# A second plain pair at the start of each feed-forward layer, and token sums formed in place

## The chip, the cores and the metric

The kernel runs on one core of a Trainium2 chip. The metric is device time in microseconds (us) of one execution. Engines are named as in the profile: PE multiplies matrices, DVE, ACT and POOL work on tiles, SP issues DMAs.

## The reference

A block of two layers over 1024 tokens of width 1024, in float32. Layer 0 mixes tokens (spatial gating and a convolution), layer 1 is dilated attention; behind each stands the feed-forward layer that the change touches:

```python
def conv_ffn(x, norm_g, w_up, conv_w, conv_b, w_down):
    h = rms_norm(x, norm_g)
    u = causal_dwconv(h @ w_up, conv_w, conv_b)      # width 3 along tokens
    gate, val = jnp.split(u, 2, axis=-1)             # 2 x 2816 channels
    return x + (jax.nn.silu(gate) * val) @ w_down
```

## The kernel before

**One product in three.** Every float32 matrix is held as a high and a low part (`hi_of`: ACT's cast; `lo_of`: a subtraction, mostly on DVE), and a product of 128 x 128 weights with 512 tokens is three matmuls into one PSUM bank: high by high, high weights by low tokens, low weights by high tokens. The third is the first that needs the low part of the weights. All DVE and POOL instructions are issued through one helper, so that they have line L115; hi_of has L183.

**The up stage.** The 2816 gate and 2816 value channels are worked through in 22 pairs of 128 gate and 128 value channels. The normed activations `hT` have four blocks, token half t by half b of the width 1024 (`hT.block(t, b)`), each of a high and a low tile (`hTh`, `hTl`). A pair is a product of 2 x 2 blocks of weights (gate, value by b) with 2 x 2 blocks of tokens. It exists in two forms:

- *plain* (`plain`, `up_units`): all eight block products, as four units (gate or value, by token half) of 24 matmuls each into a `psu` bank. It needs the two weight tiles `wr` split into `wh` and `wl`, and `hT`.
- *seven products* (`Pair`, Strassen's scheme in Winograd's form): `p12` (two products with `hT.block(0, ...)`, banks `psb` and `psa`), `p6`, `p57`, `p4` with token sums T[2], T[1] and T[3], T[4], and `p3` with `hT.block(1, 1)`. Each product is 12 matmuls (lines L929, L930, L932). It needs weight sums, made by `plan` in steps (gate parts a1; four POOL sums s12, s3, s4; then the parts of s12, s3, s4), three snapshots `sn` of a bank on ACT and three additions on DVE.

The token sums are formed once a layer out of the transposed norms `xr` (`hT.raw`): `t_sums(i)` adds up token tile i with tile i + 4, and `t_parts(i, m)` splits sum m of that tile into T[m] (`t1h`, `t1l` and so on; the low part of T[4] on POOL, the others on DVE).

Then `Conv.put` forms the bias and the last tap on ACT (`y`, L810) and the other taps on DVE out of the bank; a bank of the first token half is held until the second half's taps are done. `gate` multiplies Silu(gate) by value and stores it.

**What sets the order.** The program is written as one sequence for all engines: a `Ticker` counts steps (a step follows every 6 matmuls), `after(n, f)` puts `f` n steps later, and `until` runs steps until something has been issued. Each engine carries out its own instructions in the order written, and waits on semaphores. So moving an `after` moves an instruction in its engine's queue and nothing else.

At the start of a layer the last norms (8 token tiles, `norm_tile`) are still under way. Before, pair 0 is plain and pairs 1 and 2 are the first of the seven-product form: pair 0's units of the first token half, `p12` of pair 1, all four tiles' `t_sums`, pair 0's units of the second half, `p12` of pair 2, then the sums' products of pairs 1 and 2 in turn; from pair 3 on a loop in which `p4` and `p3` of a pair follow `p12` of the next.

Of the kernel before, what the change touches and what calls it, by code (L numbers as in the profile page):

```python
# [21 lines left out]
HALF = 512  # L22
# [7 lines left out]
NPAIR = D_FF // P  # L30
# [30 lines left out]
LEADS = (4, 6)  # L61

START_AT = 8


class Ticker:
# [56 lines left out]
def block_kernel(ctx, tc, io, out):  # L123
# [5 lines left out]
    tk = Ticker()  # L129
    vec = Meter(nc.vector, 0.12, 1.06e-3)  # L130
    pool = Meter(nc.gpsimd, 0.12, 2.25e-3)
    tk.hooks.append(lambda: (vec.step(1.28), pool.step(1.3)))
    after, tick = tk.after, tk.tick
# [16 lines left out]
    def stile(shape=(P, D), dt=F32, name="s"):  # L150
        return spool.tile(list(shape), dt, tag="s", name=nm(name))
# [30 lines left out]
    def hi_of(hi, src):  # L182
        nc.scalar.copy(hi, src)  # L183

    def lo_of(lo, src, hi, eng=None):
        (eng or vec).tensor_tensor(lo, src, f32v(hi), op=ALU.subtract)
# [206 lines left out]
    def up_units(hT, ws, outs, done=None, early=False):  # L393

        if early:
            yield from first_half(hT, ws, outs)
            for n in range(len(ws)):
                after(1, lambda n=n: done(n, 0))
        for t in range(1 if early else 0, 2):
            x = hT.wait(t)  # L400
            for n, (wh, wl) in enumerate(ws):
                whv = wh.rearrange("p (k c) -> p k c", k=KT)
                wlv = wl.rearrange("p (k c) -> p k c", k=KT)
                ps = bank("psu")
                outs[(n, t)] = ps
                for k in range(KT):
                    mm3(ps, (whv[:, k, :], wlv[:, k, :]), x(k), k == 0, k == KT - 1)
                    if k == KT - 1 and done is not None:
                        after(1, lambda n=n, t=t: done(n, t))
                    if k % 2 == 1:  # L410
                        yield

    def drive(gen):
        for _ in gen:
            tick()
# [380 lines left out]
    def ffn_up(l, acts):  # L796
        fcw = param("fcw", [P, 2 * NPAIR, 3], l)
        fcb = param("fcb", [P, 2 * NPAIR], l)
        raws = {}
        first = []  # L800

        def fetch(j):
            if j < NPAIR:
                raws[j] = (stile(name="wr"), stile(name="wr"))
                for n in range(2):
                    src = io["w_up"][l, j + n * NPAIR].rearrange("p k c -> p (k c)")
                    nc.sync.dma_start(raws[j][n], src)
# [45 lines left out]
            return part.rearrange("p (k c) -> p k c", k=4)  # L853


        def start():
            fetch(0)

            def part():
                hi, lo = stile(dt=F32R, name="wh"), stile(dt=F32R, name="wl")  # L860
                raw = raws[0][len(first)]
                hi_of(hi, raw)
                after(1, lambda hi=hi, lo=lo, raw=raw: lo_of(lo, raw, hi))
                first.append((hi, lo))
            after(START_AT, part)
            after(START_AT + 2, part)
            after(START_AT + 4, lambda: fetch(1))

        def plain(hT):
            tk.until(lambda: len(first) == 2 and 1 in raws)  # L870
            cv, outs = Conv(0), {}
            return up_units(hT, first, outs, lambda n, t: cv.put(n, t, outs[(n, t)]))


        prep = {}
# [4 lines left out]
            after(1, lambda: lo_of(lo, src, hi))  # L880
            return hi, lo

        def plan(j, lead, lag=0):


            if j >= NPAIR:
                return
            o = prep[j] = {}

            def two(t):  # L890
                return t.rearrange("p (b c) -> p b c", b=2)

            def gate_parts():
                g = two(raws[j][0])
                o["a1"] = split_s(g)

            def sums():
                g, v = two(raws[j][0]), two(raws[j][1])
                s12, s4 = stile([P, 2, HALF], name="s12"), stile([P, 2, HALF], name="s4")
                o["s12r"], o["s4r"] = s12, s4  # L900
                pool.tensor_tensor(s12[:, 0, :], v[:, 0, :], v[:, 1, :], op=ALU.add)
                pool.tensor_tensor(s12[:, 1, :], s12[:, 0, :], g[:, 0, :], op=ALU.subtract)
                pool.tensor_tensor(v[:, 0, :], g[:, 0, :], v[:, 0, :], op=ALU.subtract)
                pool.tensor_tensor(s4[:, 0, :], g[:, 1, :], s12[:, 1, :], op=ALU.subtract)

            def s12_parts():
                o["s12"] = split_s(o["s12r"])

            def s3_parts():
                o["s3"] = split_s(two(raws[j][1]))  # L910

            def s4_parts():
                hl = stile([P, 2, HALF], F32R, name="w4")
                hi_of(hl[:, 0, :], o["s4r"][:, 0, :])
                after(1, lambda: lo_of(hl[:, 1, :], o["s4r"][:, 0, :], hl[:, 0, :]))
                o["s4"] = hl
            after(lead - 6 + lag // 3, gate_parts)
            after(lead - 5 + lag, sums)
            after(lead + 1 + lag, s12_parts)
            after(lead + 5 + lag, s3_parts)  # L920
            after(lead + 9 + lag, s4_parts)

        def product(ps, a, b, first, last):
            (ah, al), (bh, bl) = a, b
# [11 lines left out]
        T, sums = {}, {}  # L936
        tails = deque()

        def t_sums(hT, i):

            r0, r1 = hT.raw[i], hT.raw[i + 4]
            ta = stile([P, 2, HALF], name="ta")
            vec.tensor_tensor(ta[:, 0, :], r1[:, 0, :], r0[:, 0, :], op=ALU.subtract)
            vec.tensor_tensor(ta[:, 1, :], r1[:, 1, :], ta[:, 0, :], op=ALU.subtract)
            pool.tensor_tensor(r1[:, 0, :], r1[:, 1, :], r1[:, 0, :], op=ALU.subtract)
            pool.tensor_tensor(r0[:, 1, :], r0[:, 1, :], ta[:, 1, :], op=ALU.subtract)
            sums[i] = {1: ta[:, 0, :], 2: ta[:, 1, :], 3: r1[:, 0, :], 4: r0[:, 1, :]}

        def t_parts(i, m):

            if m not in T:
                T[m] = operand(f"t{m}")
            hi, lo = T[m]
            c = slice(i * P, (i + 1) * P)
            v = sums[i][m].rearrange("p (k t) -> p k t", k=4)
            split(v, hi[:, :, c], lo[:, :, c], pool if m == 4 else None)

        class Pair:
# [7 lines left out]
                self.sn[key] = stile([P, HALF], name="sn")  # L966
                nc.scalar.copy(self.sn[key], self.b)  # L967

            def p12(self, late=0):
                self.b, self.a = bank("psb"), bank("psa")  # L970
                product(self.b, self.part("a1", 0), self.hT.block(0, 0), True, True)
                after(1, lambda: self.snap("p1"))
                product(self.a, self.part("a1", 1), self.hT.block(0, 1), True, True)

                def c11():
                    vec.tensor_tensor(self.a, self.a, self.sn["p1"], op=ALU.add)
                    after(1, lambda: self.cv.put(0, 0, self.a))
                after(1 + late, c11)

            def p6(self):  # L980
                product(self.b, self.part("s12", 1), T[2], False, True)
# [28 lines left out]
                after(1, c12)  # L1010

        def run(hT):

            gen = plain(hT)
            plan(1, 8, 10)
            after(4, lambda: fetch(2))
            for _ in range(8):
                next(gen)
                tick()
            one, two = Pair(1, hT), None  # L1020
            plan(2, 12, 5)
            after(18, lambda: fetch(3))
            one.p12()
            hT.wait(1)
            for i in range(4):
                after(1 + i, lambda i=i: t_sums(hT, i))
            for n, m in enumerate((2, 1, 3, 4)):
                for i in range(4):
                    after(4 + (4 * n + i) * 3 // 4, lambda i=i, m=m: t_parts(i, m))
            drive(gen)  # L1030
            two = Pair(2, hT)
            two.p12(5)
            plan(3, 16)
            one.p6()
            one.p57()
            two.p6()
            one.p4()
            one.p3()
            two.p57()
            tails.extend((two.p4, two.p3))  # L1040
            for j in range(3, NPAIR):
                plan(j + 1, 14)
                after(4, lambda j=j: fetch(j + 2))
                if j == 3:
                    fetch(4)
                p = Pair(j, hT)
                p.p12()
                while tails:
                    tails.popleft()()
                p.p6()  # L1050
                p.p57()
                tails.extend((p.p4, p.p3))
            return tails
# [527 lines left out]
    hT = Normed()  # L1581
# [133 lines left out]
```

## Time and profile before

| | us |
|---|---|
| three runs | 2329.06 (median), 2328.94, 2331.13 |
| the profiled execution | 2330.07 |
| its span in the trace | 2328.3 |

Rows of instructions read: start, duration, engine, line, operation, output<-inputs (buffer numbers left out), shapes, count; in brackets how long the engine had been idle before and what ended that. A matmul's duration is its latency; matmuls overlap, so PE's pace is the distance between starts. In the tables of windows the columns are the length, then the busy time and number of instructions of each engine, the granted clock of PE (1.00 is full speed), and the DMA engines' share and rate.

### The profile page before, as it was taken

What the parts mean: (1) busy time and instruction counts of PE and PEld (TensorE: products, weight loads), DVE (VectorE), ACT (ScalarE), POOL (GpSimd) and SP (SyncE); (2) the same over time, 40 slices, a digit from 0 to 9 for tenths busy, and PEclk for the clock granted to TensorE, in tenths of its full rate; (3) what the DMA queues carried; (4) which work ended last, traced back from release to release, by engine and by line L of the source; (5) the groups of instructions that cost most, each with busy time, mean ns of one, the idle gap of its engine ahead of it and who ended that gap; (6) DMA issues with size and microseconds to landing.
All of it is one profiled execution on the core that took longest, in us unless ns stands there. A gap on an engine that the chain in (4) does not pass through costs nothing. (4 is left out here: it accounts for less than half of the span.)

```text
span 2328.3 us, 28663 instructions
## 1 busy us (share of the span) xinstructions
PE 2235.6 (96%) x10616; PEld 1863.7 (80%) x10616; DVE 1585.4 (68%) x2530; ACT 1078.1 (46%) x1648; POOL 461.9 (20%) x387
## 2 busy tenths in 40 slices
PE   7998888999999999999999999999899999999998
PEld 6886676888888888887888888787678888888887
DVE  6977759877777743425777777776887777774352
ACT  4356265444444533323555555654544444454140
POOL 1022136233333002010000000122633333310000
PEclk9999889999999999999999999999999999999999
DMA  5389611222222563525344444723122222247260
GB/s 200 87 145 220 167 76 52 83 89 87 87 85 68 178 247 130 205 89 132 97 112 111 114 118 118 226 64 110 46 90 82 82 82 82 82 156 278 71 245 36
DMA packets 87884, 281.23 MB, mean 121 GB/s; under 512 B 12352, under 2 KB 12736, under 8 KB 87744
## 3 DMA queue, kind: packets, MB, share of 16 engines
q1 hardware_dynamic: 80976, 254.91, 33.4%
q0 software_dynamic: 6768, 24.49, 5.5%
q8 instruction: 83, 1.36, 0.2%
q14 instruction: 57, 0.47, 0.1%
HBM read 180.88 MB, written 64.92 MB: 106 GB/s over the span
## 5 line engine op out<-in xcount | busy, mean ns | idle before, releaser
L244 PE MATMUL psd<-w,ah 128*128 128x512 f32 x704 | 274.3, 390 | 0.0
L246 PE MATMUL psd<-w,al 128*128 128x512 f32 x704 | 273.9, 389 | 0.0
L245 PE MATMUL psd<-w,ah 128*128 128x512 f32 x704 | 273.9, 389 | 0.0
L244 PE MATMUL psu<-hTh,w 128*128 128x512 f32 (+1 forms) x592 | 237.1, 400 | 9.3 <-ACT w L183 9.0
L246 PE MATMUL psu<-hTh,w 128*128 128x512 f32 (+1 forms) x592 | 229.8, 388 | 0.0
L245 PE MATMUL psu<-hTl,w 128*128 128x512 f32 (+1 forms) x592 | 229.3, 387 | 0.2 <-DVE hTl L115 0.2
L115 DVE TENSOR_TENSOR x<-psd,x 128x512 f32<-128x512 f32 x128 | 86.4, 686 | 183.4 <-PE psd L246 182.8
L115 DVE TENSOR_TENSOR w<-wr,w 128x1024 fp32r<-128x1024 f32 x142 | 177.8, 1262 | 44.6 <-ACT w L183 42.9
L183 ACT CAST w<-wr 128x1024 fp32r<-128x1024 f32 x144 | 149.9, 1050 | 60.3 <-PE psd L246 30.9
L115 POOL TENSOR_TENSOR sm<-sm,mhalf 128x1 f32<-128x1 f32 (+2 forms) x46 | 32.0, 696 | 651.1 <-DVE sm L115 651.1
L246 PEld LDWEIGHTS psd<-w,al 128*128 128x128 f32 x704 | 132.2, 188 | 27.7
L244 PEld LDWEIGHTS psd<-w,ah 128*128 128x128 f32 x704 | 132.2, 188 | 27.2
L245 PEld LDWEIGHTS psd<-w,ah 128*128 128x128 f32 x704 | 132.2, 188 | 27.1
L115 POOL TENSOR_TENSOR s<-wr 128x512 f32<-128x512 f32 x42 | 56.9, 1355 | 486.1 <-DMA act<-y 359.5
L244 PEld LDWEIGHTS psu<-hTh,w 128*128 128x128 f32 x592 | 112.7, 190 | 26.8 <-ACT w L183 9.4
L115 DVE TENSOR_TENSOR tt<-ppt,tt 128x512 fp32r<-128x512 f32 (+1 forms) x160 | 101.3, 634 | 46.1 <-ACT tt L183 45.0
L183 ACT CAST tt<-ppt 128x512 fp32r<-128x512 f32 (+1 forms) x160 | 86.6, 541 | 97.7 <-PE ppt L1350 88.0
L246 PEld LDWEIGHTS psu<-hTh,w 128*128 128x128 f32 x592 | 112.1, 189 | 23.8 <-DVE w L115 0.8
L115 DVE TENSOR_TENSOR wl<-wr,wh 128x1024 fp32r<-128x1024 f32 x88 | 129.8, 1475 | 0.2 <-ACT wh L183 0.2
L245 PEld LDWEIGHTS psu<-hTl,w 128*128 128x128 f32 x592 | 112.7, 190 | 17.6 <-DVE hTl L115 0.5
L1299 ACT ACTIVATE p<-p,sma 128x896 f32<-128x896 f32 (+7 forms) x128 | 99.5, 778 | 35.6 <-DVE sma L115 33.7
L967 ACT COPY sn<-psb 128x512 f32<-128x512 f32 x126 | 73.3, 582 | 86.9 <-PE psb L932 83.6
(229 smaller groups left out, 5816.3 us busy)
## 6 DMA issues: line engine op xcount, KB each, us to landing
wr<-in_w_up_dram SPq DMA_DIRECT2D x88, 512.0 KB, 5.0
wr<-in_w_down_dram SPq DMA_DIRECT2D x88, 512.0 KB, 7.5
act<-y SPq DMA_DIRECT2D x44, 512.0 KB, 3.0
ar<-act SPq DMA_DIRECT2D x88, 256.0 KB, 6.9
wr<-in_w_qkv_dram SPq DMA_DIRECT2D x24, 512.0 KB, 3.9
x<-in_x_dram SPq DMA_DIRECT2D x16, 512.0 KB, 10.1
x_ffn<-x SPq DMA_DIRECT2D x16, 512.0 KB, 2.6
x<-x_ffn SPq DMA_DIRECT2D x16, 512.0 KB, 8.3
```

What stands on the lines that cost most here:

```text
L115: return fn(*args, **kw)
L183: nc.scalar.copy(hi, src)
L244: nc.tensor.matmul(out_ap, st[0], mv[0], start=first, stop=False)
L245: nc.tensor.matmul(out_ap, st[0], mv[1], start=False, stop=False)
L246: nc.tensor.matmul(out_ap, st[1], mv[0], start=False, stop=last)
L967: nc.scalar.copy(self.sn[key], self.b)
L1299: nc.scalar.activation(p, p, AF.Exp, bias=sm[:, 2:3], scale=0.125, accum_out=lsum[hp][:, c:c + 1])
```

## The change

`N_PLAIN = 2`: pairs 0 and 1 are both plain. Pair 1's weights are split from step 2 on; the seven-product form begins with pair 2, and its weights are prepared with other lead times. `t_sums` works in place in the `xr` tiles, with three subtractions on DVE and one on POOL (before: two on each, and a tile `ta`), and is issued for tile i three steps after the norm of tile i + 4, by a hook (`as_they_come`), not after all norms. `t_parts` are spread over 24 steps rather than 12. The special order of pairs 1 and 2 is gone.

```diff
+N_PLAIN = 2
...
+        def first_part(j):
+            hi, lo = stile(dt=F32R, name="wh"), stile(dt=F32R, name="wl")
+            raw = raws[j][len(first[j])]
+            hi_of(hi, raw)
+            after(1, lambda: lo_of(lo, raw, hi))
+            first[j].append((hi, lo))
...
-        def plain(hT):
-            tk.until(lambda: len(first) == 2 and 1 in raws)
-            cv, outs = Conv(0), {}
-            return up_units(hT, first, outs, lambda n, t: cv.put(n, t, outs[(n, t)]))
+        def plain(j, hT):
+            tk.until(lambda: len(first[j]) == 2)
+            cv, outs = Conv(j), {}
+            return up_units(hT, first[j], outs, lambda n, t: cv.put(n, t, outs[(n, t)]))
...
-            after(lead - 6 + lag // 3, gate_parts)
-            after(lead - 5 + lag, sums)
-            after(lead + 1 + lag, s12_parts)
-            after(lead + 5 + lag, s3_parts)
-            after(lead + 9 + lag, s4_parts)
+            after(lead - 6 - early, gate_parts)
+            after(lead - 5, sums)
+            after(lead + 1, s12_parts)
+            after(lead + 5, s3_parts)
+            after(lead + 9, s4_parts)
...
             r0, r1 = hT.raw[i], hT.raw[i + 4]
-            ta = stile([P, 2, HALF], name="ta")
-            vec.tensor_tensor(ta[:, 0, :], r1[:, 0, :], r0[:, 0, :], op=ALU.subtract)
-            vec.tensor_tensor(ta[:, 1, :], r1[:, 1, :], ta[:, 0, :], op=ALU.subtract)
-            pool.tensor_tensor(r1[:, 0, :], r1[:, 1, :], r1[:, 0, :], op=ALU.subtract)
-            pool.tensor_tensor(r0[:, 1, :], r0[:, 1, :], ta[:, 1, :], op=ALU.subtract)
-            sums[i] = {1: ta[:, 0, :], 2: ta[:, 1, :], 3: r1[:, 0, :], 4: r0[:, 1, :]}
+            vec.tensor_tensor(r0[:, 0, :], r1[:, 0, :], r0[:, 0, :], op=ALU.subtract)
+            vec.tensor_tensor(r1[:, 0, :], r1[:, 1, :], r1[:, 0, :], op=ALU.subtract)
+            vec.tensor_tensor(r1[:, 1, :], r1[:, 1, :], r0[:, 0, :], op=ALU.subtract)
+            pool.tensor_tensor(r0[:, 1, :], r0[:, 1, :], r1[:, 1, :], op=ALU.subtract)
+            sums[i] = {1: r0[:, 0, :], 2: r1[:, 1, :], 3: r1[:, 0, :], 4: r0[:, 1, :]}
...
         def run(hT):
-
-            gen = plain(hT)
-            plan(1, 8, 10)
-            after(4, lambda: fetch(2))
-            for _ in range(8):
-                next(gen)
-                tick()
-            one, two = Pair(1, hT), None
-            plan(2, 12, 5)
-            after(18, lambda: fetch(3))
-            one.p12()
+            tk.until(lambda: 1 in raws)
+            for n in range(2):
+                after(2 + 2 * n, lambda: first_part(1))
+            after(10, lambda: fetch(2))
+            gens, seen = [], [0]
+
+            def as_they_come():
+                while seen[0] < hT.done[1]:
+                    after(3, lambda i=seen[0]: t_sums(hT, i))
+                    seen[0] += 1
+            tk.hooks.append(as_they_come)
+            for j in range(N_PLAIN):
+                gens.append(plain(j, hT))
+                for _ in range(8):
+                    next(gens[j])
+                    tick()
             hT.wait(1)
-            for i in range(4):
-                after(1 + i, lambda i=i: t_sums(hT, i))
+            as_they_come()
+            tk.hooks.remove(as_they_come)
             for n, m in enumerate((2, 1, 3, 4)):
                 for i in range(4):
-                    after(4 + (4 * n + i) * 3 // 4, lambda i=i, m=m: t_parts(i, m))
-            drive(gen)
-            two = Pair(2, hT)
-            two.p12(5)
-            plan(3, 16)
-            one.p6()
-            one.p57()
-            two.p6()
-            one.p4()
-            one.p3()
-            two.p57()
-            tails.extend((two.p4, two.p3))
-            for j in range(3, NPAIR):
+                    after(2 + (4 * n + i) * 3 // 2, lambda i=i, m=m: t_parts(i, m))
+            plan(N_PLAIN, 16, 3)
+            after(12, lambda: fetch(3))
+            for gen in gens:
+                drive(gen)
+            for j in range(N_PLAIN, NPAIR):
```

In the rows of order that follow, the names are tiles with their numbers; the lines of the changed kernel are two higher (L117 is the helper of DVE and POOL).

On PE, behind pair 0's second unit of the first token half. Before, pair 1's first seven-form product follows:

```order
L244 MATMUL psu_2715<-hTh_2382,wh_2318 128x512
L245 MATMUL psu_2715<-hTl_2383,wh_2318 128x512
L246 MATMUL psu_2715<-hTh_2382,wl_2319 128x512
L929 MATMUL psb_2765<-hTh_2378,wh_2722 128x512
L930 MATMUL psb_2765<-hTl_2379,wh_2722 128x512
L932 MATMUL psb_2765<-hTh_2378,wl_2723 128x512
```

Now:

```order
L246 MATMUL psu_2722<-hTh_2382,wh_2318 128x512
L247 MATMUL psu_2722<-hTl_2383,wh_2318 128x512
L248 MATMUL psu_2722<-hTh_2382,wl_2319 128x512
L246 MATMUL psu_2777<-hTh_2378,wh_2669 128x512
L247 MATMUL psu_2777<-hTl_2379,wh_2669 128x512
L248 MATMUL psu_2777<-hTh_2378,wl_2670 128x512
```

Pair 1's two units of the first half stand there now (48 matmuls, where 24 of `p12` stood), and behind them all four units of the second half.

On DVE, from the end of the last norm (`xn`) on. Before, the last tile's low parts hTl come after two taps of pair 0 and a low part of weights, and the sums (`ta`) after those:

```order
L115 SCALAR_TENSOR_TENSOR xn_2669<-x_1699,sm_2670,gb_2231 128x1024
L115 SCALAR_TENSOR_TENSOR y_2711<-psu_2638,fcw_2223,y_2711 128x511
L115 SCALAR_TENSOR_TENSOR y_2711<-psu_2638,fcw_2223,y_2711 128x510
L115 TENSOR_TENSOR wl_2723<-wr_2341,wh_2722 128x1024
L115 TENSOR_TENSOR hTl_2607<-xr_2754,hTh_2606 128x4x128
L115 TENSOR_TENSOR hTl_2611<-xr_2754,hTh_2610 128x4x128
L115 SCALAR_TENSOR_TENSOR y_2761<-psu_2715,fcw_2223,y_2761 128x511
L115 SCALAR_TENSOR_TENSOR y_2761<-psu_2715,fcw_2223,y_2761 128x510
L115 TENSOR_TENSOR psa_2766<-psa_2766,sn_2785 128x512
L115 TENSOR_TENSOR ta_2807<-xr_2603,xr_2375 128x512
```

Now, behind the norm and the first tile's three sums:

```order
L117 SCALAR_TENSOR_TENSOR y_2718<-psu_2638,fcw_2223,y_2718 128x511
L117 SCALAR_TENSOR_TENSOR y_2718<-psu_2638,fcw_2223,y_2718 128x510
L117 TENSOR_TENSOR xr_2435<-xr_2662,xr_2435 128x512
L117 TENSOR_TENSOR xr_2662<-xr_2662 128x512
L117 TENSOR_TENSOR xr_2662<-xr_2662,xr_2435 128x512
L117 TENSOR_TENSOR wl_2708<-wr_2342,wh_2707 128x1024
L117 TENSOR_TENSOR xr_2491<-xr_2700,xr_2491 128x512
L117 TENSOR_TENSOR xr_2700<-xr_2700 128x512
L117 TENSOR_TENSOR xr_2700<-xr_2700,xr_2491 128x512
L117 TENSOR_TENSOR hTl_2607<-xr_2766,hTh_2606 128x4x128
L117 TENSOR_TENSOR hTl_2611<-xr_2766,hTh_2610 128x4x128
```

Nine sums of three tiles stand ahead of the last tile's hTl; before, none did.

On DVE, ahead of the first operand of a seven-form pair that PE waited for. Before, it was the low part of pair 2's gate weights (wl_2834), behind eight sums and two t2l:

```order
L115 TENSOR_TENSOR ta_2836<-xr_2696,xr_2491 128x512
L115 TENSOR_TENSOR ta_2836<-xr_2696,ta_2836 128x512
L115 TENSOR_TENSOR ta_2847<-xr_2754,xr_2547 128x512
L115 TENSOR_TENSOR ta_2847<-xr_2754,ta_2847 128x512
L115 TENSOR_TENSOR t2l_2853<-ta_2807,t2h_2852 128x4x128
L115 TENSOR_TENSOR t2l_2853<-ta_2818,t2h_2852 128x4x128
L115 TENSOR_TENSOR wl_2834<-wr_2703,wh_2833 128x1024
```

Now, up to the low part of pair 2's s12 (wl_3018), for its product with T[2]:

```order
L117 TENSOR_TENSOR t3l_2982<-xr_2603,t3h_2981 128x4x128
L117 TENSOR_TENSOR y_2773<-y_2718,y_2773 128x1024
L117 TENSOR_TENSOR t3l_2982<-xr_2662,t3h_2981 128x4x128
L117 SCALAR_TENSOR_TENSOR y_2839<-psu_2814,fcw_2223,y_2839 128x1
L117 SCALAR_TENSOR_TENSOR y_2839<-psu_2968,fcw_2223,y_2839 128x511
L117 SCALAR_TENSOR_TENSOR y_2839<-psu_2814,fcw_2223,y_2839 128x2
L117 SCALAR_TENSOR_TENSOR y_2839<-psu_2968,fcw_2223,y_2839 128x510
L117 TENSOR_TENSOR t3l_2982<-xr_2700,t3h_2981 128x4x128
L117 TENSOR_TENSOR t3l_2982<-xr_2766,t3h_2981 128x4x128
L117 TENSOR_TENSOR wl_3018<-s_410_2945,wh_3017 128x1024
L117 TENSOR_TENSOR psa_3008<-psa_3008,sn_3035 128x512
L117 TENSOR_TENSOR y_2839<-y_2810,y_2839 128x1024
```

The low part of s12 stands behind the taps of the eighth plain unit (psu_2968) and the last t3l; the gate low part of pair 2 has moved forward, between the first t1l and the taps of the sixth unit.

More of the change, by code (lines that the diff above doesn't have):

```diff
@@ L799, in ffn_up @@
         raws = {}
-        first = []
+        first = [[] for _ in range(N_PLAIN)]
         def fetch(j):
@@ L853, in view @@
             return part.rearrange("p (k c) -> p k c", k=4)
+        def first_part(j):
[4 more added lines that the diff above has]
+            first[j].append((hi, lo))
         def start():
             fetch(0)
[L859 to L866, printed above, removed]
+            after(START_AT, lambda: first_part(0))
+            after(START_AT + 2, lambda: first_part(0))
             after(START_AT + 4, lambda: fetch(1))
-        def plain(hT):
-            tk.until(lambda: len(first) == 2 and 1 in raws)
-            cv, outs = Conv(0), {}
-            return up_units(hT, first, outs, lambda n, t: cv.put(n, t, outs[(n, t)]))
+        def plain(j, hT):
+            tk.until(lambda: len(first[j]) == 2)
+            cv, outs = Conv(j), {}
+            return up_units(hT, first[j], outs, lambda n, t: cv.put(n, t, outs[(n, t)]))
         prep = {}
@@ L881, in split_s, with plan @@
             return hi, lo
-        def plan(j, lead, lag=0):
+        def plan(j, lead, early=0):
             if j >= NPAIR:
@@ L967, in snap, with p12 @@
                 nc.scalar.copy(self.sn[key], self.b)
-            def p12(self, late=0):
+            def p12(self):
                 self.b, self.a = bank("psb"), bank("psa")
@@ L977, in c11 @@
                     after(1, lambda: self.cv.put(0, 0, self.a))
-                after(1 + late, c11)
+                after(1, c11)
             def p6(self):
@@ L1012, in run @@
         def run(hT):
-            gen = plain(hT)
-            plan(1, 8, 10)
-            after(4, lambda: fetch(2))
-            for _ in range(8):
-                next(gen)
-                tick()
-            one, two = Pair(1, hT), None
-            plan(2, 12, 5)
-            after(18, lambda: fetch(3))
-            one.p12()
+            tk.until(lambda: 1 in raws)
[13 more added lines that the diff above has]
+                    tick()
             hT.wait(1)
-            for i in range(4):
-                after(1 + i, lambda i=i: t_sums(hT, i))
+            as_they_come()
+            tk.hooks.remove(as_they_come)
             for n, m in enumerate((2, 1, 3, 4)):
                 for i in range(4):
-                    after(4 + (4 * n + i) * 3 // 4, lambda i=i, m=m: t_parts(i, m))
-            drive(gen)
-            two = Pair(2, hT)
-            two.p12(5)
-            plan(3, 16)
-            one.p6()
-            one.p57()
-            two.p6()
-            one.p4()
-            one.p3()
-            two.p57()
-            tails.extend((two.p4, two.p3))
-            for j in range(3, NPAIR):
+                    after(2 + (4 * n + i) * 3 // 2, lambda i=i, m=m: t_parts(i, m))
[4 more added lines that the diff above has]
+            for j in range(N_PLAIN, NPAIR):
                 plan(j + 1, 14)
                 after(4, lambda j=j: fetch(j + 2))
-                if j == 3:
-                    fetch(4)
                 p = Pair(j, hT)
```

## The prediction

> **What bounds the kernel now.** I read the page first, then the waits of PE and its rows in order of time where they stand, then windows around them, and last the queues of DVE, ACT and POOL there. The page: engine totals, and PE and its granted clock in 40 slices of 58 us.
>
> ```profile
> span 2328.3 us, 28663 instructions
> PE 2235.6 (96%) x10616; PEld 1863.7 (80%) x10616; DVE 1585.4 (68%) x2530; ACT 1078.1 (46%) x1648; POOL 461.9 (20%) x387
> ...
> PE   7998888999999999999999999999899999999998
> ...
> PEclk9999889999999999999999999999999999999999
> ```
>
> PE sets the pace. Of the slices in which it falls to 8, 6 and 28 (counted from 0; 349 to 407 us and 1630 to 1688) hold the starts of the two feed-forward layers; 3 to 5 lie in the mixing stage, which the change leaves alone. The windows (columns as in their head: length, then busy time and count of PE, PEld, DVE, ACT, POOL, clock, DMA) run from the first product of pair 1 to the first product of pair 3 in each layer; the third is the steady stretch behind.
>
> ```profile
> core 0: us, PE busy (x) PEld busy (x) DVE busy (x) ACT busy (x) POOL busy (x), PEclk, DMA share, GB/s
> 364.54:425.66 61.12, 49.92 (x193) 39.12 (x192) 58.01 (x60) 27.18 (x42) 38.56 (x23) 0.89 0.18 61
> 1650.44:1712.36 61.92, 50.23 (x193) 39.61 (x192) 56.34 (x60) 28.40 (x42) 38.54 (x23) 0.89 0.18 60
> 425.66:520.00 94.34, 94.34 (x417) 77.92 (x416) 70.31 (x100) 44.36 (x60) 30.25 (x20) 1.00 0.21 73
> ```
>
> In the first two DVE is busy 58.01 of 61.12 us and 56.34 of 61.92: there DVE is the bound and PE waits for it. In the third PE never waits. PE's rows (start, duration, line, tiles, idle before and what ended it), layer 0 and then layer 1:
>
> ```profile
> 364.54 0.39 PE L929 MATMUL psb<-hTh,wh 128*128 128x512 f32 x1
> ...
> 381.09 0.39 PE L930 MATMUL psb<-hTl,wh 128*128 128x512 f32 x1
> 387.28 0.80 PE L932 MATMUL psb<-hTh,wl 128*128 128x512 f32 x1 [5.80 <-DVE wl L115]
> 387.87 0.63 PE L929 MATMUL psb<-hTh,wh 128*128 128x512 f32 x1
> 388.30 0.63 PE L930 MATMUL psb<-hTl,wh 128*128 128x512 f32 x1
> ...
> 401.74 0.49 PE L929 MATMUL psb<-t3h,wh 128*128 128x512 f32 x1 [0.63 <-ACT sn L967]
> 405.03 0.51 PE L930 MATMUL psb<-t3l,wh 128*128 128x512 f32 x1 [2.80 <-DVE t3l L115]
> 407.24 0.80 PE L932 MATMUL psb<-t3h,wl 128*128 128x512 f32 x1 [1.70 <-DVE wl L115]
> ...
> 425.66 0.39 PE L929 MATMUL psb<-hTh,wh 128*128 128x512 f32 x1
> ...
> 428.38 0.39 PE L929 MATMUL psa<-hTh,wh 128*128 128x512 f32 x1
> ```
> ```profile
> 1650.44 0.40 PE L929 MATMUL psb<-hTh,wh 128*128 128x512 f32 x1
> ...
> 1673.20 0.79 PE L932 MATMUL psb<-hTh,wl 128*128 128x512 f32 x1 [5.80 <-DVE wl L115]
> ...
> 1712.36 0.39 PE L929 MATMUL psb<-hTh,wh 128*128 128x512 f32 x1
> ```
>
> A product is 12 matmuls; 425.66 to 428.38 is one, so a matmul takes 2.72 / 12 = 0.2267 us of PE at full clock (the 0.39 is its latency). Behind the 5.80 us wait starts are 0.43 apart (387.87, 388.30): the clock had halved. The 192 matmuls of the first window need 192 x 0.2267 = 43.52 us and take 61.12: 17.60 lost, 11.20 as idle PE (61.12 - 49.92) and 6.40 to the halved clock. In layer 1, 18.40 are lost.
>
> **The change on PE.** Pair 1 gets eight block products of 12 matmuls instead of seven: +12 matmuls a layer. In the order of the changed kernel PE runs four units of 24 on the second half's tokens where it had two, before it first needs a product of token sums. If nothing is late, the stretch from 364.54 to the first product of pair 3 is 204 x 0.2267 = 46.24 us. Against the trace: 61.12 - 46.24 = 14.88 gained in layer 0, 61.92 - 46.24 = 15.68 in layer 1, 30.56 together; what the 24 added matmuls cost (5.44) is in it. From pair 3 on every queue holds what it held, and PE is 94.34 of 94.34 us busy, so what is gained there moves all that follows forward.
>
> **What can be late.** The sum now hangs on operands that DVE makes. Its rows:
>
> ```profile
> 360.73 1.28 DVE L115 SCALAR_TENSOR_TENSOR xn<-x,sm,gb 128x1024 f32<-128x1024 f32 x1
> 361.93 1.53 DVE L115 SCALAR_TENSOR_TENSOR y<-psu,fcw,y 128x511 f32<-128x511 f32 x2
> ...
> 370.86 0.68 DVE L115 TENSOR_TENSOR ta<-xr,xr 128x512 f32<-128x512 f32 x1
> 371.58 0.69 DVE L115 TENSOR_TENSOR ta<-xr,ta 128x512 f32<-128x512 f32 x1
> 372.19 1.78 DVE L115 TENSOR_TENSOR ta<-xr,xr 128x512 f32<-128x512 f32 x1
> ...
> 386.01 1.21 DVE L115 TENSOR_TENSOR wl<-wr,wh 128x1024 fp32r<-128x1024 f32 x1
> 387.14 1.78 DVE L115 SCALAR_TENSOR_TENSOR y<-psu,fcw,y 128x1 f32<-128x1 f32 x4
> 388.83 1.28 DVE L115 TENSOR_TENSOR t2l<-ta,t2h 128x512 fp32r<-128x512 f32 x2
> ...
> 404.89 2.29 DVE L115 TENSOR_TENSOR wl<-wr,wh 128x1024 fp32r<-128x1024 f32 x1
> 407.10 2.29 DVE L115 TENSOR_TENSOR y<-y,y 128x1024 f32<-128x1024 f32 x1
> ```
> ```profile
> 357.64 0.55 POOL L115 TENSOR_TENSOR sm<-sm,mhalf 128x1 f32<-128x1 f32 x1 [4.01 <-DVE sm L115]
> 362.15 1.28 POOL L115 TENSOR_TENSOR s<-wr 128x512 f32<-128x512 f32 x1 [3.96 <-DVE xn L115]
> ...
> 373.38 1.73 POOL L115 TENSOR_TENSOR xr<-xr,ta 128x512 f32<-128x512 f32 x1
> ...
> 397.75 6.67 POOL L115 TENSOR_TENSOR t4l<-xr,t4h 128x512 fp32r<-128x512 f32 x4
> ```
>
> Alone, a 512-wide subtraction holds DVE 0.61 us (371.58 to 372.19), 0.72 where the next one needs its result (370.86 to 371.58), a 1024-wide low part 1.13, a pair of taps 1.44, four taps 1.69 (start to start). Beside a POOL operation two-source SBUF work takes 1.78 instead of 0.68 and 2.29 instead of 1.21: 1.1 us more. Taps read PSUM and stay at 1.53.
>
> A tile's sums: DVE three in a chain, 0.72 + 0.72 + 0.61 = 2.05, where it had two; POOL one, where it had two. Of pair 1's preparation, POOL's four weight sums go, on DVE three low parts, w4 and three additions against two low parts, on ACT three snapshots, three casts and w4's against two casts. In all a layer has 1 instruction less on DVE, 5 on ACT, 8 on POOL. SP issues the same DMAs, with one activation store earlier.
>
> I follow DVE's new queue from 361.93, where it ends the last norm in both. Sums of tile 4 to 363.98, taps 365.42, tile 5's sums 367.47, the second low part of pair 1 at 368.6 (369.7 beside POOL). PE reaches its third matmul, which needs it, at 364.54 + 26 x 0.2267 = 370.4: no wait. Tile 6's sums and the two hTl of tile 7 with two POOL delays: 374.1, wanted at 375.7. Taps, tile 7's sums and two pairs of taps: 380.4; two t2l 382.8; four taps 384.5; two t2l, a t1l and pair 2's first low part with three POOL delays: 390.7, wanted at 397.6. Then 8 taps, three t1l, two t3l and a gate of 1.13 take 7.6: 398.3. The last four taps need the eighth unit, which ends at 397.4, and the base on ACT:
>
> ```profile
> 356.23 1.06 ACT L309 ACTIVATE xn<-x 128x1024 f32<-128x1024 f32 x1 [1.11 <-DVE x L115]
> 359.94 1.05 ACT L183 CAST wh<-wr 128x1024 fp32r<-128x1024 f32 x1
> ...
> 390.48 0.77 ACT L810 ACTIVATE y<-psu,fcb,fcw 128x512 f32<-128x512 f32 x1
> ...
> 1674.92 1.28 ACT L844 ACT_TABLE_LOAD   x1 [3.63 <-DVE y L115]
> ```
>
> so 398.2 at the earliest. Taps to 400.0, two t3l 401.2, and the low part of s12 (wl_3018 in the order) at 402.4. PE wants it at 364.54 + 170 x 0.2267 = 403.1. This is what is late next: the slack is 0.7 us. Between 0 and 1.5 us of wait (the end with all eight POOL operations delaying DVE: 33.9 us of queue plus 8 x 1.1 from 361.93 is 404.6); I take 0.3, near the lower end, since six of those eight delays are already counted and POOL's t4l cannot start before ACT has cast t4h. In layer 1 the first Silu brings the table load quoted, ahead of the t1h casts; by it DVE comes up to 1.1 later there, so 0.4 late, which the 0.3 covers. Next, the s3 low part: an addition 0.6, a gate and itself at 2.29 beside t4l: 408.0, wanted at 408.5; 0. Next, pair 3's first low part: taps 1.44 and 1.13 to 2.29, so 410.6 to 411.7, wanted at 411.2: 0 to 0.5, I take 0.2.
>
> Two insertions lie ahead of 361.93. ACT's cast for pair 1 (1.05) stands before the last Square, where ACT idled 1.11: free, and if that gap is gone 1.05 late. DVE's low part of 1.13 stands beside POOL's root seed (0.55), on which the last norm waits; DVE idled there for hTh, so 0 to 0.6, I take 0.3, straight onto PE's last transposes:
>
> ```profile
> 362.29 1.04 PE L346 MATMUL psn<-ident,xn 128*128 128x128 f32 x8
> ```
>
> ACT's queue has 27.18 busy of 61.12 us and loses five instructions: nothing, unless a snapshot comes to stand behind a Silu, some 1 us. POOL, 38.56 busy, loses eight: nothing.
>
> New waits: 0.3 + 0.3 + 0.2 = 0.8 a layer, 1.6 in all. Sum: -30.56 + 1.6 = -29.0. The profiled execution took 2330.07, so 2301.1 for one like it; the median shown is 1.0 lower, so 2300.
>
> The Trainium skill, "SBUF — State Buffer", section "Who interferes with whom", says that a DVE instruction with two SBUF inputs and a GpSimd instruction that reads SBUF take one interface in turn and the later one is blocked for the whole instruction. The rows agree in kind (1.78 against 0.68). By that rule as an estimate each delay could be a whole POOL operation, 1.28, so eight give 10.2, the s12 low part 406.0, 3 us late a layer, and a time of about 2306.
>
> **Rivals.** First, contention at its worst: DVE and POOL meet at all eight operations and again at t4l. s12's low part comes at 405.7, 2.6 late, pair 3's 0.5, the norm 0.6: 3.7 a layer, 7.4 in all, 2306. For it: DVE has hardly any slack in its queue and each of these meetings can be seen in the present rows. Against: POOL has eight operations less, and waits for PE before its weight sums. A wait long enough to halve the clock (5.80 did it; how much less would do, the rows don't show) adds some 11 matmuls x 0.2 = 2.2 a layer, up to 2310.
>
> Second, slower: DVE becomes so late at s12's product that PE loses more than the 14.88 gained. It decides when DVE's queue up to there is over 15 us longer than mine. If all 30 two-source operations ran at the contended price, the queue would be 33.9 + 33 = 66.9, the low part at 428.8, 25.7 late, and with 2.2 of slow clock each layer 13 us longer: 2355. Against: a delay needs a POOL operation, and there are eight, and four of t4l.
>
> Third, the change does not do what it says: the earlier end of the up stage is lost again in the down stage or attention, 2329. For it: PE waits there too. Against: those waits are for norms and conversions that move along, and no DMA release among PE's.
>
> **How the numbers follow.** Forecast 2298 to 2303: 0.69. Contention, to 2310: 0.25. Slower 0.03, unchanged 0.03. So faster by over 0.2% (4.7 us, about what a measurement tells here) 0.94, same 0.03, slower 0.03. Range: no new wait at all gives 2328.94 - 30.56 = 2298.4, with 0.9 for the rest of the program 2297.5; the upper end is the contention case without the slow clock and a little more, 2307.
>
> **What would show it.** Right: no 5.80 us wait for wl in PE's rows; from the first psu of pair 1 to the first psb of pair 3 about 47 us in both layers; about 24 more matmuls, 2 DVE, 10 ACT and 16 POOL instructions less; slices 6 and 28 of PE at 9. The first wait left is at the product of t2h and the s12 low part, below 1 us. Wrong: a wait there of several us, hTl of tile 7 behind the sums, or the halved clock again.

## The result, and the profile after

The changed kernel takes 2300.06 us (median of four runs, 2297.75 to 2301.03), the kernel before, run beside it, 2329.53 (2328.94 to 2331.13): a ratio of 0.9871, 95% interval 0.9854 to 0.9888. The profiled execution of the changed kernel took 2297.75, with a span of 2295.9. Lines of DVE's and POOL's helper are now L117, of a seven-form product L931, L932 and L934, of a plain unit L246 to L248.

The page after, the rows that answer to those of before:

```profile
span 2295.9 us, 28656 instructions
PE 2228.1 (97%) x10640; PEld 1861.3 (81%) x10640; DVE 1564.4 (68%) x2528; ACT 1072.3 (47%) x1638; POOL 434.7 (19%) x371
...
PE   7998889999999999999999999999999999999998
...
PEclk9999999999999999999999999999999999999999
```

PE has 24 matmuls more and is busy 7.5 us less: what the halved clock had stretched is gone. Slices 6 and 28 stand at 9. DVE has 2 instructions less, ACT 10, POOL 16, as counted.

The windows from pair 1's first product to pair 3's first product, layer 0 and layer 1, with the columns of before:

```profile
core 0: us, PE busy (x) PEld busy (x) DVE busy (x) ACT busy (x) POOL busy (x), PEclk, DMA share, GB/s
363.43:409.67 46.24, 46.24 (x205) 38.29 (x204) 43.80 (x57) 22.45 (x35) 21.45 (x14) 1.00 0.27 89
1633.16:1679.43 46.27, 46.27 (x206) 38.30 (x205) 42.88 (x57) 23.65 (x35) 20.92 (x14) 1.00 0.27 91
```

PE is busy for the whole of both windows at full clock, 204 matmuls in 46.24 us, where 192 took 61.12 and 61.92. DVE is still busy 43.80 of the 46.24 us: it is close to binding again. PE's rows at the joints, layer 0, and then layer 1:

```profile
361.17 1.04 PE L348 MATMUL psn<-ident,xn 128*128 128x128 f32 x8
...
363.43 0.39 PE L246 MATMUL psu<-hTh,wh 128*128 128x512 f32 x1
...
401.97 0.39 PE L934 MATMUL psb<-t2h,wl 128*128 128x512 f32 x1
...
410.49 0.50 PE L934 MATMUL psb<-hTh,wl 128*128 128x512 f32 x1 [0.20 <-DVE wl L117]
...
1680.24 0.50 PE L934 MATMUL psb<-hTh,wl 128*128 128x512 f32 x1 [0.20 <-DVE wl L117]
```

The 5.80 us wait has gone, and so have those for t3l and for the snapshot. The last norm (psn) and the product of t2h with the low part of s12 wait for nothing; 0.20 us is left at pair 3's first low part. DVE's rows that the sum hung on, in layer 0 and (the last) in layer 1:

```profile
367.57 1.78 DVE L117 TENSOR_TENSOR xr<-xr,xr 128x512 f32<-128x512 f32 x1
...
370.71 2.37 DVE L117 TENSOR_TENSOR hTl<-xr,hTh 128x512 fp32r<-128x512 f32 x2
...
375.90 0.69 DVE L117 TENSOR_TENSOR xr<-xr,xr 128x512 f32<-128x512 f32 x1
...
382.48 2.98 DVE L117 TENSOR_TENSOR t2l<-xr,t2h 128x512 fp32r<-128x512 f32 x2
385.39 1.78 DVE L117 TENSOR_TENSOR t1l<-xr,t1h 128x512 fp32r<-128x512 f32 x1
...
397.09 1.79 DVE L117 SCALAR_TENSOR_TENSOR y<-psu,fcw,y 128x1 f32<-128x1 f32 x4 [1.26 <-ACT y L812]
...
400.00 1.22 DVE L117 TENSOR_TENSOR wl<-s,wh 128x1024 fp32r<-128x1024 f32 x1
...
1669.74 1.22 DVE L117 TENSOR_TENSOR wl<-s,wh 128x1024 fp32r<-128x1024 f32 x1
```

The low part of s12 ends at 400.00 + 1.22 = 401.22; PE wants it at 401.97, so 0.75 us are to spare.

The two windows give (61.12 - 46.24) + (61.92 - 46.27) = 30.53 us, and the spans of the two profiled executions differ by 32.4. The other 1.9 lies outside, where the instructions are almost the same: executions differ there by more than that (pair 1's first product in layer 0, ahead of which the work is almost the same, falls between 363.2 and 366.8 us in the runs below). The medians differ by 29.5.

### The profile page after: what moved, and what is told of

Its sections match the earlier page's. It is cut to its first block, busy times and chain, and to the rows that moved or that the text cites. A ratio compares the mean times of both kernels' runs of the same rounds, so it can differ in the third digit from the quotient of the medians.

```text
span 2295.9 us, 28656 instructions
## 1 busy us (share of the span) xinstructions
PE 2228.1 (97%) x10640; PEld 1861.3 (81%) x10640; DVE 1564.4 (68%) x2528; ACT 1072.3 (47%) x1638; POOL 434.7 (19%) x371
## 5 line engine op out<-in xcount | busy, mean ns | idle before, releaser
L246 PE MATMUL psd<-w,ah 128*128 128x512 f32 x704 | 274.3, 390 | 0.0
L248 PE MATMUL psd<-w,al 128*128 128x512 f32 x704 | 273.9, 389 | 0.0
L247 PE MATMUL psd<-w,ah 128*128 128x512 f32 x704 | 273.9, 389 | 0.0
L246 PE MATMUL psu<-hTh,w 128*128 128x512 f32 (+1 forms) x592 | 236.9, 400 | 8.5 <-ACT w L185 8.2
L248 PE MATMUL psu<-hTh,w 128*128 128x512 f32 (+1 forms) x592 | 229.4, 388 | 0.0
L247 PE MATMUL psu<-hTl,w 128*128 128x512 f32 (+1 forms) x592 | 229.0, 387 | 0.2 <-DVE hTl L117 0.2
L117 DVE TENSOR_TENSOR x<-psd,x 128x512 f32<-128x512 f32 x128 | 86.5, 687 | 182.8 <-PE psd L248 182.3
L117 DVE TENSOR_TENSOR w<-wr,w 128x1024 fp32r<-128x1024 f32 x142 | 178.0, 1264 | 42.8 <-ACT w L185 41.4
L117 POOL TENSOR_TENSOR sm<-sm,mhalf 128x1 f32<-128x1 f32 (+2 forms) x46 | 33.8, 734 | 649.7 <-DVE sm L117 649.7
L248 PEld LDWEIGHTS psd<-w,al 128*128 128x128 f32 x704 | 132.1, 188 | 27.6
L247 PEld LDWEIGHTS psd<-w,ah 128*128 128x128 f32 x704 | 132.2, 188 | 27.3
L246 PEld LDWEIGHTS psd<-w,ah 128*128 128x128 f32 x704 | 132.2, 188 | 27.1
L117 POOL TENSOR_TENSOR s<-wr 128x512 f32<-128x512 f32 x40 | 54.0, 1350 | 437.7 <-DMA act<-y 358.2
L246 PEld LDWEIGHTS psu<-hTh,w 128*128 128x128 f32 x592 | 112.2, 190 | 26.0 <-ACT w L185 8.6
L117 DVE TENSOR_TENSOR tt<-ppt,tt 128x512 fp32r<-128x512 f32 (+1 forms) x160 | 101.3, 634 | 46.3 <-ACT tt L185 45.2
L117 DVE TENSOR_TENSOR wl<-wr,wh 128x1024 fp32r<-128x1024 f32 x88 | 132.8, 1509 | 0.0
L248 PEld LDWEIGHTS psu<-hTh,w 128*128 128x128 f32 x592 | 111.9, 189 | 23.8 <-DVE w L117 0.8
L247 PEld LDWEIGHTS psu<-hTl,w 128*128 128x128 f32 x592 | 112.4, 190 | 17.5 <-DVE hTl L117 0.5
L1366 PE MATMUL po<-tt,v 128*128 128x256 f32 x640 | 108.5, 291 | 5.0 <-DVE tt L117 3.4
```

The costliest lines, as they stand in the source:

```text
L117: return fn(*args, **kw)
L246: nc.tensor.matmul(out_ap, st[0], mv[0], start=first, stop=False)
L247: nc.tensor.matmul(out_ap, st[0], mv[1], start=False, stop=False)
L248: nc.tensor.matmul(out_ap, st[1], mv[0], start=False, stop=last)
L1366: nc.tensor.matmul(po[:, c], v2[:, kb, :], tt[:, z, 256 * n:256 * n + 256], start=(g == 0 and n == 0 and z == 0), stop=(g == j and n == 1 ...
```

## The experiments

Three questions: which part of the change brings the gain, by what, and what is left. Each ratio is to the kernel before, run beside it. "Stretch" is the window above in layer 0 / layer 1; for kernels with two plain pairs it is 46.24 us when nothing waits, with one 43.52.

| plain pairs | token sums | us, median | ratio, 95% interval | stretch |
|---|---|---|---|---|
| 1 | late, with ta (before) | 2329.53 | 1 | 61.12 / 61.92 |
| 1 | early, in place | 2324.93 | 0.9980 (0.9970 to 0.9989) | 58.21 / 58.33 |
| 1 | the same, pair 1's gate parts earlier | 2322.46 | 0.9969 (0.9959 to 0.9980) | 57.04 / 57.15 |
| 2 | late, with ta | 2321.59 | 0.9966 (0.9953 to 0.9979) | 57.15 / 57.73 |
| 2 | late, in place | 2322.32 | 0.9967 (0.9955 to 0.9979) | 56.98 / 57.55 |
| 2 | early, with ta | 2320.86 | 0.9961 (0.9947 to 0.9976) | 56.72 / 56.37 |
| 2 | early, in place (the changed kernel) | 2300.06 | 0.9871 (0.9854 to 0.9888) | 46.24 / 46.27 |
| 2 | the same, buffers of ta taken and freed at once | 2301.79 | 0.9873 (0.9856 to 0.9889) | 46.24 / 47.20 |
| 2 | the same, buffers of ta held | 2321.56 | 0.9964 (0.9951 to 0.9977) | 56.93 / 57.09 |

**The second plain pair alone** (the sums of before, after all norms). The edit also puts back `t_sums` with `ta`; the part on the order is:

```diff
-            tk.hooks.append(as_they_come)
...
-            as_they_come()
-            tk.hooks.remove(as_they_come)
+            for i in range(4):
+                after(1 + i, lambda i=i: t_sums(hT, i))
```

> Two plain pairs as in the changed kernel, token sums as before (two DVE and two POOL subtractions with the tile ta, issued after all norms). Theory, the 48 matmuls that PE has ahead cover DVE's preparation and the form of the sums matters little: 2299 to 2303 us, the stretch from pair 1's first product to pair 3's first product 46.2 to 48 us in both layers, no wait above 1.5 us in it. Rival A, the sums (one POOL operation instead of two, formed earlier) bring the gain: 2320 to 2330, waits of several us for wl again. Rival B, both parts are needed: between, 2306 to 2320.

2321.59 us, 8.8 less than the kernel before beside it (2330.39): the theory is wrong. The time lies in rival A's range, and above rival B's; the next run, with the sums alone, rules A out and leaves B (both parts are needed). PE waits at the T[2] product, first for a snapshot on ACT:

```profile
407.71 0.80 PE L931 MATMUL psb<-t2h,wh 128*128 128x512 f32 x1 [6.24 <-ACT sn L969]
410.88 0.80 PE L934 MATMUL psb<-t2h,wl 128*128 128x512 f32 x1 [1.95 <-DVE wl L117]
```

From pair 1's first product to the first sum product PE has 168 matmuls now and had 96 before. These 72 more (the expectation had said 48) do not cover DVE.

**The sums alone** (the edit of t_sums and the hook, in the order of before):

> The order of before with one plain pair, only the sums changed (three DVE and one POOL subtraction in place, three steps after each norm). Theory: PE still comes to pair 2's gate low part with too few matmuls ahead; DVE's queue up to there has 4 x 0.65 us more and 4 POOL operations less, so the wait of 5.8 us stays within 3 to 8 us and the clock is halved behind it: 2325 to 2333. Rival A, the sums bring the gain: 2300 to 2310.

2324.93 us, 0.07 below the theory's range and far above the rival's: the sums alone don't bring the gain. The wait of 5.80 us has split up; PE's rows that wait most in layer 0:

```profile
368.39 0.80 PE L932 MATMUL psb<-hTh,wl 128*128 128x512 f32 x1 [3.58 <-DVE wl L115]
...
394.65 0.50 PE L932 MATMUL psb<-t2h,wl 128*128 128x512 f32 x1 [2.76 <-DVE wl L115]
```

The first is new: pair 1's low part stands behind two tiles' sums. So that place was mended too:

```diff
-            after(lead - 6 + lag // 3, gate_parts)
+            after(lead - 6 if j == 1 else lead - 6 + lag // 3, gate_parts)
```

> One plain pair, sums in place as they come, and pair 1's gate parts three steps earlier, so that its low part no longer stands behind two tiles' sums on DVE (3.58 and 3.75 us of PE's wait with the sums alone). Theory, with one plain pair PE has too few matmuls ahead of the sum products whatever the order: the wait comes back at the low part of s12 and behind, 2319 to 2325. Rival, that one place was what spoiled the early sums, and a second plain pair isn't needed: 5.3 us gained in each layer, 2312 to 2316.

2322.46 us, as the theory had it: the 3.58 is gone, and in layer 0 PE now waits mainly 0.94, 2.25, 1.43 and 1.57 us for low parts that DVE makes, and 1.07 for a snapshot. With one plain pair DVE was late in each order tried. Each against the kernel before run beside it, the second plain pair alone gave 8.8 us and the sums alone 5.5 (7.8 with the gate parts earlier); both together gave 29.5, far more than their sum.

**Sums in place, but late** (only the hook undone):

> The changed kernel with the in-place sums issued after all norms, not as they come. Theory: DVE's work up to s12's low part is the same and its end is set by the eighth unit's taps (DVE idles 1.26 us for ACT's base before them), so 2299 to 2302 and the stretch within 0.5 us of 46.24. Rival, the early sums fill idle time of DVE and are needed: s12's low part up to 3 us later a layer, a wait of about 2 us there, 2304 to 2306.

2322.32 us: the theory is wrong, the rival right in kind but not in size. DVE's rows in layer 0 show why:

```profile
365.60 1.53 DVE L117 SCALAR_TENSOR_TENSOR y<-psu,fcw,y 128x511 f32<-128x511 f32 x2
370.79 1.53 DVE L117 SCALAR_TENSOR_TENSOR y<-psu,fcw,y 128x511 f32<-128x511 f32 x2 [3.66 <-ACT y L812]
376.23 1.53 DVE L117 SCALAR_TENSOR_TENSOR y<-psu,fcw,y 128x511 f32<-128x511 f32 x2 [3.91 <-ACT y L812]
377.68 0.68 DVE L117 TENSOR_TENSOR xr<-xr,xr 128x512 f32<-128x512 f32 x1
...
409.50 2.30 DVE L117 TENSOR_TENSOR wl<-s,wh 128x1024 fp32r<-128x1024 f32 x1
```

The tiles that the sums read are complete, but the sums stand behind taps that wait for PE's units. DVE idles 3.66 + 3.91 us and begins the sums at 377.68, when in the changed kernel the last one on DVE is done (375.90 + 0.69 = 376.59): there they fill that idle time. The low part of s12 ends 411.80 - 364.32 = 47.48 us behind pair 1's first product, where it was 401.22 - 363.43 = 37.79. PE's rows (1.62 us were lost ahead of them, at pair 2's first low part), and ACT's:

```profile
408.68 0.79 PE L931 MATMUL psb<-t2h,wh 128*128 128x512 f32 x1 [4.19 <-ACT sn L968]
411.85 0.80 PE L934 MATMUL psb<-t2h,wl 128*128 128x512 f32 x1 [1.96 <-DVE wl L117]
```
```profile
404.44 1.06 ACT L846 ACTIVATE y<-y 128x1024 f32<-128x1024 f32 x1 [6.82 <-DVE y L117]
...
408.04 0.58 ACT L968 COPY sn<-psb 128x512 f32<-128x512 f32 x1
```

The first wait is for a snapshot (sn) on ACT, which stands behind a Silu that waits 6.82 us for DVE, a base and casts. The expectation had looked at the 1.26 us that DVE idles late in the changed kernel and not at what opens up earlier when the sums leave.

**Sums early, in the form of before** (tile ta, two subtractions on DVE, two on POOL):

> The changed kernel with the sums as they come, but in before's form (tile ta, two subtractions on DVE and two on POOL). Theory, the early place in DVE's queue is what counts: the sums then run while DVE would wait for PE's units (3.66 and 3.91 us of idle with late sums), and the form is worth at most the slack at the T[2] product: 2299 to 2302, no wait above 1 us in the stretch. Rival, the in-place form is needed because four more POOL subtractions slow DVE by 1.1 us each, 4.4 a layer against 2.6 of DVE work saved: s12's low part 1 to 2 us late, 2302 to 2306.

2320.86 us: neither. 20.8 us are lost, where contention was to cost at most 6. ACT's row of the third base y, that of pair 1's first unit:

```profile
381.75 0.78 ACT L812 ACTIVATE y<-psu,fcb,fcw 128x512 f32<-128x512 f32 x1 [15.37 <-PE psu L248]
```

Its own unit was done some 11 us earlier. The tiles ta, y, wh, wl, s and xr come from one ring of 23 buffers; four ta held from the sums to the parts of T[1] may be what y lacks. Two runs took POOL's form out of it. The first only takes the buffers:

```diff
+            ta = stile([P, 2, HALF], name="ta")
+            vec.tensor_tensor(ta[:, 0, 0:1], r1[:, 0, 0:1], r0[:, 0, 0:1], op=ALU.subtract)
             vec.tensor_tensor(r0[:, 0, :], r1[:, 0, :], r0[:, 0, :], op=ALU.subtract)
```

> The changed kernel with its own sums (three DVE, one POOL, in place, as they come), but each tile's sums also take a tile ta from the ring of 23 buffers, as before's form does, and write one column of it on DVE (four small DVE instructions a layer, some 0.1 us each). Theory, what before's form costs is the four ring buffers, not its POOL subtractions: the bases y on ACT then wait for buffers that PE reads until pair 0's last units (15.37 us in layer 0 with the two-and-two form), DVE's taps stand behind them: 2316 to 2323, waits of about 4 and 2 us at the T[2] product. Rival, the two-and-two form loses by contention and DVE order: then this one stays at 2300 to 2302.

2301.79 us, the rival's range: the theory as it was written here, that taking the buffers costs the time, is wrong. Layer 0 loses nothing, in layer 1 PE waits 0.65 us for the low part of s12. But a buffer freed at once is not a buffer held, so contention had not been shown either. The next run holds the tile:

```diff
+            sums[i][0] = ta
...
+            if m == 1:
+                ta = sums[i][0]
+                vec.tensor_tensor(ta[:, 0, 1:2], ta[:, 0, 0:1], ta[:, 0, 0:1], op=ALU.subtract)
```

> As the run before this one (own sums, each tile's sums take a tile ta besides), and the tile is now read once more on DVE when T[1]'s part of that token tile is made, so that it holds its buffer as long as in before's form, 20 to 30 us instead of well under 1; again small DVE instructions of some 0.1 us. Theory, it is the four buffers held that cost 20 us in the two-and-two form: ACT's third base of the stretch waits for pair 0's gate weights (some 10 us late), 2314 to 2323. Rival, the buffers do not matter even when held, and contention of POOL's subtractions is the cause: 2300 to 2303.

2321.56 us, the theory's range: the held buffers alone, with POOL's work as in the changed kernel, cost as much as the two-and-two form. ACT's row, first of the run that frees them at once, then of the run that holds them, and DVE's of the latter:

```profile
369.43 0.78 ACT L812 ACTIVATE y<-psu,fcb,fcw 128x512 f32<-128x512 f32 x1 [4.46 <-PE psu L248]
```
```profile
382.16 0.78 ACT L812 ACTIVATE y<-psu,fcb,fcw 128x512 f32<-128x512 f32 x1 [15.35 <-PE psu L248]
```
```profile
381.93 0.16 DVE L117 TENSOR_TENSOR ta<-xr,xr 128x1 f32<-128x1 f32 x1 [4.56 <-PE psu L247]
```

Against pair 1's first product (363.79 and 365.63) the base starts at 5.64 and at 16.53 us. 16.53 is about three units of 24 matmuls (72 x 0.2267 = 16.32), the end of pair 0's first unit of the second half, which is the last to read pair 0's gate weights. Nothing in the base's own inputs changed; what it waits for is its buffer. In the program as built for this run, and for the two-and-two form too, that y takes the buffer of the low part wl of pair 0's gate weights (last read in a matmul of L248), and DVE's fourth ta that of the high part wh (last read in one of L247): the two releasers above. Behind them the waits are those of the late sums:

```profile
408.68 0.80 PE L931 MATMUL psb<-t2h,wh 128*128 128x512 f32 x1 [4.38 <-ACT sn L974]
411.85 0.80 PE L934 MATMUL psb<-t2h,wl 128*128 128x512 f32 x1 [1.95 <-DVE wl L117]
```

So with two plain pairs neither the early sums (2320.86, buffers held) nor the freed buffers (2322.32, sums late) gain over the second pair alone (2321.59); both together gain 21 us.

**A third plain pair.** Pair 2 driven whole behind the two, seven products from pair 3 on:

```diff
-        first = [[] for _ in range(N_PLAIN)]
+        first = [[] for _ in range(N_PLAIN + 1)]
...
-            plan(N_PLAIN, 16, 3)
+            for n in range(2):
+                after(6 + 2 * n, lambda: first_part(2))
             after(12, lambda: fetch(3))
+            plan(3, 32, 3)
+            after(28, lambda: fetch(4))
             for gen in gens:
                 drive(gen)
-            for j in range(N_PLAIN, NPAIR):
+            drive(plain(2, hT))
+            for j in range(3, NPAIR):
```

> A third plain pair (pair 2) after the two. Theory, nothing is left to hide in that stretch: 12 more matmuls a layer at 0.2267 us, 2.72 a layer, 5.44 in all, less at most 0.4 of waits that are left: 2304.5 to 2306, 24 more PE instructions, the stretch from pair 1's first product to pair 4's first one 68.0 us (300 matmuls) where the changed kernel has 65.3 (288). Rival, DVE is still the bound behind the stretch (operands of pairs 2 and 3 just in time): a third pair gives DVE more time and costs less than 3 us, or nothing.

2318.63 us (ratio 0.9951, 0.9937 to 0.9966): far worse than either. Pair 3's operands were late by 0.47, 2.52 and 1.36 us in layer 0, and the clock halved behind the 2.52. The row where ACT stopped:

```profile
415.28 0.62 ACT L185 CAST t4h<-xr 128x512 fp32r<-128x512 f32 x1 [17.06 <-PE psu L247]
```

L247 reads hTl. T[4]'s tiles and those of hT come from one ring of 14, and hT with all four sums would need 16; so t4h takes a buffer that the plain pairs still read. Written 15 or 16 steps later:

```diff
-                    after(2 + (4 * n + i) * 3 // 2, lambda i=i, m=m: t_parts(i, m))
+                    after(36 + i if m == 4 else 2 + (4 * n + i) * 3 // 2,
+                          lambda i=i, m=m: t_parts(i, m))
```

> Three plain pairs, with the parts of T[4] made 12 to 16 steps later. With T[4] where it was, ACT stood 17.06 us at its t4h cast for a PE read in pair 2's units, and the casts and taps behind it were late. Theory, that stop is the whole excess over the 24 added matmuls: 2304.5 to 2307, the stretch up to the first product of pair 4 68.0 to 69 us. Rival, DVE or ACT are late for another reason with a third plain pair: still above 2311, with waits of several us at pair 3's first product.

2305.86 us (0.9897, 0.9882 to 0.9911), as the theory had it. Its window up to pair 4's first product, layer 0:

```profile
363.95:431.98 68.03, 68.03 (x301) 56.32 (x300) 52.88 (x73) 28.54 (x42) 21.40 (x14) 1.00 0.25 88
```

300 matmuls without a gap, and 5.8 us more than the changed kernel. A third pair has nothing left to hide and pays for its 24 matmuls.

**How much slack is left.** In the changed kernel the low part of s12 of pair 2 is written again, 2 times in layer 0, 4 times in layer 1, in one execution:

```diff
                 o["s12"] = split_s(o["s12r"])
+                if j == N_PLAIN:
+                    hi, lo = o["s12"]
+                    for _ in range((2, 4)[l]):
+                        after(1, lambda: lo_of(lo, o["s12r"], hi))
```

> The changed kernel with the low part of pair 2's s12 written again, 2 times more in layer 0 and 4 times in layer 1 (1.13 us of DVE each alone, up to 2.2 beside POOL's t4l), right behind the first. Theory, in the changed kernel that low part ends about 0.75 us before PE wants it and DVE is again what binds: the T[2] product, or the first operand behind it, waits 1.5 to 3.7 us in layer 0 and 3.8 to 8 in layer 1, and everything up to pair 3 moves by as much; the clock halves behind waits of about 2.5 us and more, as behind 2.52 with the third plain pair, and not behind 2.05. Rival, DVE has slack of several us there: no wait in layer 0, less than 2 in layer 1.

```profile
409.08 0.80 PE L938 MATMUL psb<-t2h,wl 128*128 128x512 f32 x1 [3.57 <-DVE wl L117]
...
1688.33 0.79 PE L938 MATMUL psb<-t2h,wl 128*128 128x512 f32 x1 [6.09 <-DVE wl L117]
```

Both waits are in the theory's ranges (the execution took 2315.99 us). The three low parts of layer 0 take 5.65 us together, 4.4 more than one, and PE waits 3.57: the slack was indeed about 0.8. The stretch grows by 51.62 - 46.24 = 5.38 us, the wait and 1.81, nearly all of it halved clock; in layer 1 by 54.51 - 46.27 = 8.24, the wait and 2.15. By these sums DVE binds again there once it has some 0.8 us more to do.

## Why the prediction was right, point by point

- **The gain as matmuls against idle time.** 204 x 0.2267 = 46.24 us a stretch was forecast if nothing is late, and 46.24 and 46.27 came. This term carries the result; the medians fell by 29.5 where 29.0 was forecast.
- **DVE's queue, followed row by row.** The trace after starts the stretch 1.11 us earlier. Less that, hTl of tile 7 was forecast to be done at 373.0, the eighth unit's taps at 398.9 and s12's low part at 401.3; measured 373.08, 398.88 and 401.22. The base on ACT set the start of those taps, forecast for 397.1 at the earliest and measured at 397.09. Between these points DVE was up to 1.4 us earlier than forecast (next point but one).
- **The waits.** Sized at 0.3 (last norm), 0.3 (s12) and 0.2 (pair 3) a layer, 1.6 in all. The first two did not come. The third did, 0.20 in each layer, behind the end of the stretch. That term was too large by about 1.2 us, within the scatter of the runs.
- **Contention.** Six delays of 1.1 us on the way to s12 were counted, 6.6 us. The rows show a sum at 1.78, two hTl at 2.37, two t2l at 2.98 and a t1l at 1.78, where undelayed ones take 0.68 for one and 1.29 for two: 5.0 us. So DVE was ready for the eighth unit's taps at 395.83, not 397.2, and idled 1.26 us for the base; that idle time is why the end still came out to 0.1 us. It and the 0.75 us behind it would have hidden some 2 us more delay, but not the 3.8 more that eight full meetings would have cost. The estimate from the Trainium skill, "SBUF — State Buffer", section "Who interferes with whom" (the later instruction blocked for a whole POOL operation, s12 3 us late, 2306), is not borne out: s12's low part was not late at all.
- **The rivals.** No wait of several us, no halved clock, nothing lost again further down.
- **What the prediction did not see.** It priced the in-place form as one DVE instruction more and one POOL instruction less a tile. Its worth is another: without it four buffers are held, and 20 us of the gain are gone. The forecast held because the changed kernel has the buffers, not because it asked for them; in that it was lucky. For the same reason moving an `after` can change more than an engine's queue, against what the section on the kernel before says: if it takes a tile, it also changes which buffer a later write gets. With the tile ta and late sums the base of pair 1's first unit starts 5.64 us behind pair 1's first product, with ta and early sums 381.75 - 365.20 = 16.55. Nor did the prediction say that the early place of the sums is worth about as much as the second plain pair (without the one 22.3 us are lost, without the other 24.9): it counted the queue with the sums early and never without.

## What to carry to other kernels

When two engines run just in time, parts of a change need not add up: here each one alone left the next operand late, and only all together took the last wait away. So cost a change by following the waiting engine's queue to its end, with the parts in, and again with each one out. Look at a tile's buffers as at an engine: a tile that is held longer makes a later write wait for a reader elsewhere, and its row shows a releaser that is not one of its own inputs. Work whose inputs are ready belongs ahead of work that waits, in a queue that is carried out in order.

## What the runs showed that was not expected

A much shorter wait than 5.80 us halves PE's clock. Behind waits of 2.05 us (second plain pair alone, layer 1) and 2.25 us (one plain pair with earlier gate parts, layer 1) the matmuls went on 0.23 us apart. Behind another 2.25 us in layer 0 of that kernel they were 0.43 apart at once:

```profile
386.12 0.68 PE L932 MATMUL psb<-hTh,wl 128*128 128x512 f32 x1 [2.25 <-DVE wl L115]
386.59 0.63 PE L929 MATMUL psb<-hTh,wh 128*128 128x512 f32 x1
387.02 0.63 PE L930 MATMUL psb<-hTl,wh 128*128 128x512 f32 x1
```

So were they behind 2.52, 2.76 and 3.57 us, in part of the cases some matmuls later. And it is not the single wait alone that counts: later in the same layer they were 0.43 apart behind a wait of only 0.64 us that followed closely on one of 1.57 (starts 1.14 us apart):

```profile
402.48 0.49 PE L930 MATMUL psb<-t3l,wh 128*128 128x512 f32 x1 [1.57 <-DVE t3l L115]
403.62 0.80 PE L932 MATMUL psb<-t3h,wl 128*128 128x512 f32 x1 [0.64 <-DVE wl L115]
404.21 0.63 PE L929 MATMUL psb<-t3h,wh 128*128 128x512 f32 x1
404.64 0.63 PE L930 MATMUL psb<-t3l,wh 128*128 128x512 f32 x1
```

In the two cases where it was taken, the price hardly depends on the wait: 1.81 us behind 3.57, 2.15 behind 6.09. The Trainium skill, "TensorE: Matmul & The Clock Gate", section "Why this matters for your kernels", gives about 3 us as the idle gap to avoid. Here 2.25 us could be enough, and the same 2.25 us was once harmless.
